# A two-layer decoder trunk: plain products for the seven-product units, token-major units of 512 columns, GpSimd's arithmetic on VectorE

## Chip, cores and metric

The kernel runs on one core of a Trainium2 chip. The metric is device time in microseconds for one launch, the median of several runs; a profile is one execution recorded instruction by instruction. TensorE (PE) multiplies matrices, VectorE (DVE) and ScalarE (ACT) do elementwise work and empty the accumulators, GpSimd (POOL) does elementwise work and issues some transfers, SyncE (SP) issues the rest.

## What is computed

Two layers over 512 tokens of width 1024. In each layer one input projection feeds five branches: A, sparse attention with a top-k choice of 128 keys; B, latent attention; C, differential attention; D, a spatial gating unit with a LayerNorm; E, attention into 256 memory rows. Each branch is gated, projected and merged, and the sum is projected and added to the rows:

```python
for l in range(DEPTH):
    xn = rms_norm(h, norm_g[l])
    (a_q, a_k, a_v, i_q, i_k, i_w, b_cq, b_ckv, b_kr, c_q, c_k, c_v,
     d_u, d_v, e_q, gates, merge) = jnp.split(xn @ w_in[l], offsets, axis=-1)
    branches = (dsa_branch(...), mla_branch(...), diff_branch(...), sgu_branch(...), memory_branch(...))
    mixed = functools.reduce(jnp.add, [
        jax.nn.sigmoid(merge[:, :, n]) * ((o * jax.nn.silu(gates[:, :, n])) @ w_branch[l, n])
        for n, o in enumerate(branches)])
    h = h + mixed @ w_out[l]
return rms_norm(h, final_norm_g)
```

## The kernel before, in words

**Products.** An fp32 operand is split into two fp32r parts, hi and lo. `three` (L484) issues three matmuls for one 128-row block: hi·hi, lo·hi, hi·lo; a "triple" below. Weights come in granules of 512 KB (`gcols`, four row blocks of 256 columns), loaded by SP. For each half granule `split_steps` (L392) lets ScalarE copy the hi part (L402) and an engine subtract it for the lo part (L405): VectorE the first half, GpSimd the second.

**Units.** `unit_t` (L489) makes 256 columns of a result transposed, columns on partitions and 512 tokens in the free dimension, so its matmuls are 512 wide; gates, merges and the branch projections use it. `unit_n` (L500) makes a token-major result: the rows are the stationary operand, the weights are moved, 256 columns at a time, for four token tiles. It makes the middle columns (keys, values, indexer, latent ranks), the queries of A (`a0 a1`), queries, keys and values of C in two halves (`f0q f0k f0v f1q f1k f1v`), the two inputs of D (`dv0 dv1 du0 du1`), the memory values and the output projection. `unit_s` (L509) makes the same block as `unit_t` from half blocks in seven sums of products in place of eight, 256 wide; `seven_steps` (L363) forms the combined weights, partly on GpSimd, and `x_prep` and `x_swap` (tokens `xp`, `xs`) the combined rows. Gates and merges of A and C use it, 12 units in each layer. Their sums stand in tile `s`, of the plain units in `pm`.

**Order.** The string `ORDER` (L31) lists units and marks. `gB0` is a half of branch B's gate, `mB0` a quarter of its merge (with its quarter of the branch projection); `+dsa` starts the side stream of the sparse attention, `-dsa` and `!df0` demand that one is done. `Pace` (L58) steps the side streams at each `tick` of a triple, by estimated times; `begin` splits weights ahead. The steps are recorded in this order and then placed on each engine's own queue by the framework; an engine runs its queue in order.

**Around the change.** The indexer of A (`+idx`) makes a score tile per block of 128 tokens and takes the top values with MAX (L1061) and MATCH_REPLACE (L1062) on VectorE, 16 pairs per block for blocks 1 to 3, while PE works on branch B's gates and merges and on `f0v`. Only when all are done the sparse attention goes on: a head multiplies scores (`pS`), takes a masked softmax (custom instruction L581, ScalarE L586, reciprocal L591, ScalarE L592), transposes (`pT`), splits (`ptl`) and multiplies values (`po`), for four blocks. LayerNorm of D (`ln`, L1259) works on the tile `sguv` and has its statistics and normalisation on VectorE, gain (L1271) and offset (L1272) on GpSimd, then a split into `vnh` and `vnl`, which the product `pz` of the token `z` needs. In `gates` GpSimd multiplies gate and branch output (L1375); in `merges` it adds into the accumulators (L1411).

Of the kernel before, what the change touches and what calls it, by code (L numbers as in the profile page):

```python
# [39 lines left out]
GSET = (1,)  # L40
WSB = True
STB = True
# [15 lines left out]
class Pace:  # L58
    """Interleaves side streams (attention) with the dense products as they are traced."""
# [68 lines left out]
class Granule:  # L128
    """Up to four 128-row blocks of 256 columns of a weight, split in two fp32r parts."""

    def __init__(self, parts, n, width=256, raws=1):
        self.parts, self.n, self.width, self.raws = parts, n, width, raws


def trunk(tc, d, out, taps=None):
# [43 lines left out]
    def f32(ap):  # L179
        return ap.bitcast(F32)  # L180
# [13 lines left out]
    # ---- input rows, small vectors, constants  # L194
# [59 lines left out]
    # ---- rotary tables  # L254
# [42 lines left out]
    def rope(eng, x, j, ct, st, outs=None):  # L297
        """x [128, 2, h, 2H], token tiles 2j and 2j+1; rotated in place or into outs."""
        h, w = x.shape[2], x.shape[3]
        hf = w // 2  # L300
        tmp = tr(name="rope")
        n = 2 * h * w
        a = tmp[:, :n] if 2 * n <= 512 else tr(name="rope2")[:, :n]
        b = tmp[:, n:2 * n] if 2 * n <= 512 else tmp[:, :n]
        a, b = (z.rearrange("p (t h w) -> p t h w", t=2, h=h) for z in (a, b))

        def tb(tab, lo, hi):
            return tab[:, 2 * j:2 * j + 2, None, lo:hi].to_broadcast([128, 2, h, hi - lo])
# [9 lines left out]
    # ---- differential lambdas  # L318
# [20 lines left out]
    # ---- long lived tiles  # L339
# [7 lines left out]
    # ---- weights  # L347
    order, state = [], {"dma": 0, "split": 0, "slot": 0}

    def issue(upto):  # L350
        while state["dma"] < min(upto, len(order)):
            g = order[state["dma"]]
            g.raw = [wp.tile([128, 4, 256], F32, tag="raw", bufs=NRAW, name="raw") for _ in range(g.raws)]
            for dst, src in g.parts(*g.raw):
                nc.sync.dma_start(dst, src)
            state["dma"] += 1
# [6 lines left out]
    def seven_steps(g):  # L363
        """Seven combinations of the four 512 x 128 blocks of a granule, split, in the order of their products."""
        r0, r1 = g.raw
        a11, a21, a12, a22 = (r[:, :, c * 128:(c + 1) * 128] for r in (r0, r1) for c in range(2))
        g.prod = []

        def put(src):
            h, lo = (z.rearrange("p (k c) -> p k c", k=4) for z in wtile())  # L370
            A.activation(h, src, AF.Copy)
            yield
            (G if len(g.prod) in GSET else V).tensor_tensor(out=lo, in0=src, in1=f32(h), op=ALU.subtract)  # L373
            g.prod.append((h, lo))
            yield

        def comb(x, y, op):
            o = (blk(F32, "ws") if WSB else pp.tile([128, 512], F32, tag="p", name="ws")).rearrange(
                "p (k c) -> p k c", k=4)
            G.tensor_tensor(out=o, in0=x, in1=y, op=op)  # L380
            return o
        yield from put(a11)
        s1 = comb(a21, a22, ALU.add)
        s2 = comb(s1, a11, ALU.subtract)
        yield from put(s2)
        yield from put(comb(a11, a21, ALU.subtract))
        yield from put(s1)
        yield from put(comb(a12, s2, ALU.subtract))
        yield from put(a22)
        yield from put(a12)  # L390
# [1217 lines left out]
```

## Time and profile before

| | before |
|---|---|
| median of 3 runs | 1853.85 us (1853.25 to 1854.87) |
| span of the profiled execution | 1854.6 us |
| instructions | 31211 |
| busy PE | 1784.2 us, 96% |
| busy VectorE | 1280.2 us, 69% |
| busy ScalarE | 1000.2 us, 54% |
| busy GpSimd | 730.9 us, 39% |
| PE on the chain that ended last | 42% of the span |
| read from HBM | 155.22 MB, 86 GB/s over the span |

The rows come from the page of one execution and from its trace. "L485 PE MATMUL pm<-wh,xh" is an instruction with its line, its output and its inputs; for a token-major product the weights `wh` are the moved operand. A duration belongs to one instruction; successive matmuls overlap, so that their distance is less than their duration. In a table of stretches each engine has its busy time and its number of instructions, and PEclk is the granted clock of TensorE, 1.00 being 2.4 GHz.

### The profile page before, as it was taken

What the parts mean: (1) busy time and instruction counts of PE and PEld (TensorE: products, weight loads), DVE (VectorE), ACT (ScalarE), POOL (GpSimd) and SP (SyncE); (2) the same over time, 40 slices, a digit from 0 to 9 for tenths busy, and PEclk for the clock granted to TensorE, in tenths of its full rate; (3) what the DMA queues carried; (4) which work ended last, traced back from release to release, by engine and by line L of the source; (5) the groups of instructions that cost most, each with busy time, mean ns of one, the idle gap of its engine ahead of it and who ended that gap; (6) DMA issues with size and microseconds to landing.
All of it is one profiled execution on the core that took longest, in us unless ns stands there. A gap on an engine that the chain in (4) does not pass through costs nothing. (4 is left out here: it accounts for less than half of the span.)

```text
span 1854.6 us, 31211 instructions
## 1 busy us (share of the span) xinstructions
PE 1784.2 (96%) x11481; PEld 1613.9 (87%) x11481; DVE 1280.2 (69%) x2979; ACT 1000.2 (54%) x2247; POOL 730.9 (39%) x603
## 2 busy tenths in 40 slices
PE   7999999999999997999999999999999999899898
PEld 6998889889988777989999988898999887789888
DVE  7438656996755679899354477489775655998963
ACT  7447766437745434455355567653476454444443
POOL 4123111442312366885241321125341133778733
PEclk9999999999999998999999999999999999999999
DMA  6322222332222222334452332223322222233241
GB/s 211 92 69 78 86 69 69 97 97 70 58 58 69 80 58 69 99 95 136 131 177 58 75 89 79 57 80 103 103 58 58 58 80 58 59 91 109 85 148 69
DMA packets 167745, 161.43 MB, mean 87 GB/s; under 512 B 26036, under 2 KB 163304, under 8 KB 167592
## 3 DMA queue, kind: packets, MB, share of 16 engines
q1 hardware_dynamic: 164648, 149.21, 28.0%
q0 software_dynamic: 2944, 10.23, 1.6%
q8 instruction: 91, 1.49, 0.3%
q14 instruction: 62, 0.51, 0.1%
HBM read 155.22 MB, written 4.19 MB: 86 GB/s over the span
## 5 line engine op out<-in xcount | busy, mean ns | idle before, releaser
L405 POOL TENSOR_TENSOR wl<-raw,wh 128x512 fp32r<-128x512 f32 (+1 forms) x226 | 300.8, 1332 | 803.8 <-ACT wh L402 632.8
L402 ACT ACTIVATE wh<-raw 128x512 fp32r<-128x512 f32 (+1 forms) x460 | 285.3, 623 | 328.1 <-PE pm L486 161.6
L485 PE MATMUL pm<-wh,xh 128*128 128x256 f32 x1024 | 294.6, 288 | 0.9 <-ACT nat L1091 0.8
L486 PE MATMUL pm<-wl,xh 128*128 128x256 f32 x1024 | 293.3, 286 | 0.0
L487 PE MATMUL pm<-wh,xl 128*128 128x256 f32 x1024 | 293.2, 286 | 0.0
L405 DVE TENSOR_TENSOR wl<-raw,wh 128x512 fp32r<-128x512 f32 (+1 forms) x234 | 182.7, 782 | 144.5 <-ACT wh L402 140.1
L485 PE MATMUL pm<-xh,wh 128*128 128x512 f32 x656 | 259.2, 396 | 0.8 <-ACT mth L1392 0.5
L487 PE MATMUL pm<-xh,wl 128*128 128x512 f32 x656 | 256.9, 394 | 0.0
L486 PE MATMUL pm<-xl,wh 128*128 128x512 f32 x656 | 256.7, 391 | 0.0
L485 PEld LDWEIGHTS pm<-wh,xh 128*128 128x128 f32 x1024 | 195.1, 190 | 5.8 <-ACT nat L1091 1.6
L487 PEld LDWEIGHTS pm<-wh,xl 128*128 128x128 f32 x1024 | 195.2, 191 | 2.8 <-issue 1.7
L486 PEld LDWEIGHTS pm<-wl,xh 128*128 128x128 f32 x1024 | 195.3, 191 | 2.7 <-issue 1.2
L586 ACT ACTIVATE p<-p,nm 128x512 f32<-128x512 f32 (+1 forms) x192 | 107.2, 558 | 78.2 <-DVE nm L584 77.3
L485 PEld LDWEIGHTS pm<-xh,wh 128*128 128x128 f32 x656 | 123.7, 189 | 26.8 <-ACT mth L1392 1.1
L487 PEld LDWEIGHTS pm<-xh,wl 128*128 128x128 f32 x656 | 123.6, 188 | 26.5
L486 PEld LDWEIGHTS pm<-xl,wh 128*128 128x128 f32 x656 | 123.7, 189 | 23.8
L485 PE MATMUL s<-xh,wh 128*128 128x256 f32 x384 | 113.1, 295 | 25.2 <-ACT mth L1392 12.2
L485 PE MATMUL pm<-yh,wh 128*128 128x512 f32 x320 | 125.9, 394 | 5.3 <-DVE st L528 5.3
L486 PE MATMUL pm<-yl,wh 128*128 128x512 f32 x320 | 126.0, 394 | 0.0
L487 PE MATMUL pm<-yh,wl 128*128 128x512 f32 x320 | 122.6, 392 | 0.0
L486 PE MATMUL s<-xl,wh 128*128 128x256 f32 x384 | 111.4, 290 | 0.0
L487 PE MATMUL s<-xh,wl 128*128 128x256 f32 x384 | 110.6, 291 | 0.0
(378 smaller groups left out, 4756.5 us busy)
## 6 DMA issues: line engine op xcount, KB each, us to landing
raw<-w_in SPq DMA_DIRECT2D x192, 512.0 KB, 3.7
raw<-w_branch SPq DMA_DIRECT2D x40, 512.0 KB, 3.5
raw<-mem_w_kv SPq DMA_DIRECT2D x16, 512.0 KB, 5.6
raw<-w_out SPq DMA_DIRECT2D x16, 512.0 KB, 3.7
raw<-mla_w_uq SPq DMA_DIRECT2D x18, 128.0 KB, 2.7
xrow<-x SPq DMA_DIRECT2D x4, 512.0 KB, 7.9
raw<-mla_w_ukv SPq DMA_DIRECT2D x16, 128.0 KB, 2.7
h<-x POOLq DMA_DIRECT2D x4, 512.0 KB, 4.6
```

The lines of the kernel that those rows point to most:

```text
L402: A.activation(hv, raw, AF.Copy)
L405: (G if a else V).tensor_tensor(out=lv, in0=raw, in1=f32(hv), op=ALU.subtract)
L485: T.matmul(o, ah, bh, start=st, stop=False)
L486: T.matmul(o, ah, bl, start=False, stop=False)
L487: T.matmul(o, al, bh, start=False, stop=sp)
L586: A.activation(p[:, :L], p[:, :L], AF.Exp, bias=nm, scale=scale, accum_out=s)
```

## The change

- `unit_s`, `seven_steps`, `gseven`, `x_prep`, `x_swap` and the tokens `xp` and `xs` go; gates and merges of A and C are plain `unit_t`.
- `unit_w` takes the place of nearly all `unit_n`: 512 columns at a time, one accumulator for each of the four token tiles, granules of two row blocks of 512 columns (`gwide`), a result handed on token tile by token tile. Four middle units become two, `a0 a1` become `a`, C's values `fv`, its queries and keys `f0` (256 query and 256 key columns) and `f1`; `dv`, `du`, the memory values and the first half of the output projection are single units too. The second half of it stays at 256.
- The second subtract of each granule, the gate product, the accumulator add, LayerNorm's gain and offset and the final gain go from GpSimd to VectorE.
- `fv` and `dv` stand ahead of `f0`; the pool of 512-column tiles has 35 instead of 36 buffers, that of short-lived ones 8 instead of 6.

```diff
-ORDER = ("-mem gE0 !ckvt !lat qr q0 !qr0 gE1 k0 v0 +mla0 mE0 q1 k1 mE1 -mla0 !qr1 v1 +mla1 mE2 mE3 a0 -mla1 +idx a1 "
-         "gB0 gB1 mB0 mB1 mB2 mB3 !aq +dsa ws f0v dv0 dv1 f0q f0k z du0 du1 -dsa !df0 +df0 f1q f1k f1v -df0 !oD !df1 "
-         "gD0 gD1 +df1 mD0 mD1 -df1 mD2 xp mD3 !xp xs gA0 gA1 mA0 mA1 mA3 mA2 gC0 gC1 mem mC0 mC1 mC3 mC2")
+ORDER = ("-mem gE0 !ckvt !lat qr q0 !qr0 gE1 k0 v0 +mla0 mE0 q1 k1 mE1 -mla0 !qr1 v1 +mla1 mE2 mE3 a -mla1 +idx "
+         "gB0 gB1 mB0 mB1 mB2 mB3 !aq +dsa ws fv dv f0 z du -dsa !df0 +df0 f1 -df0 !oD !df1 "
+         "gD0 gD1 +df1 mD0 mD1 -df1 mD2 mD3 gA0 gA1 mA0 mA1 mA3 mA2 gC0 gC1 mem mC0 mC1 mC3 mC2")
-NB = 36
+NB = 35
-NTR = 6
+NTR = 8
...
     def split_steps(g):
...
-        for a in range(0, g.n, 2):
+        for a in range(0, g.n, g.per):
...
-            (G if a else V).tensor_tensor(out=lv, in0=raw, in1=f32(hv), op=ALU.subtract)
+            V.tensor_tensor(out=lv, in0=raw, in1=f32(hv), op=ALU.subtract)
...
+    def gwide(w, k0, *c0s):
+        def parts(raw):
+            r = w[k0 * 128:(k0 + 2) * 128, :].rearrange("(k p) c -> p k c", p=128)
+            cw = 512 // len(c0s)
+            return [(raw[:, :, i * cw:(i + 1) * cw], r[:, :, c0:c0 + cw]) for i, c0 in enumerate(c0s)]
+        g = Granule(parts, 2, 512)
...
-    def unit_s(g, xb, evac):
-        """Transposed 256 columns by 512 tokens in seven products of half blocks instead of eight."""
...
+    def unit_w(gs, lh, ll, evac, nt=4):
+        def run():
+            ps = [None] * nt
+            for n, g in enumerate(gs):
+                begin(g)
+                for t in range(nt):
+                    if n == 0:
+                        ps[t] = psm()
+                    for a in range(2):
+                        kt = 2 * n + a
+                        three(ps[t], lh(kt, t), ll(kt, t), g.h[a][:, 0], g.l[a][:, 0], kt == 0, kt == 2 * len(gs) - 1)
+                        tick(3 * 512 * 0.43)
+                    if n == len(gs) - 1:
+                        evac(t, ps[t])
         plan.append(run)
...
+        def diff_v():
...
+            unit_w(ww(C_CV), tk(xh), tk(xl), ev)
...
-                    G.tensor_tensor(out=v, in0=v, in1=S["lng"], op=ALU.mult)
-                    G.tensor_tensor(out=v, in0=v, in1=S["lnb"], op=ALU.add)
+                    V.tensor_tensor(out=v, in0=v, in1=S["lng"], op=ALU.mult)
+                    V.tensor_tensor(out=v, in0=v, in1=S["lnb"], op=ALU.add)
...
-                    G.tensor_tensor(out=sg, in0=sg, in1=oT[nm][k], op=ALU.mult)
+                    V.tensor_tensor(out=sg, in0=sg, in1=oT[nm][k], op=ALU.mult)
...
-                if seven:
-                    unit_s(gseven(w, c0), xb, lambda ps, u=u: ev(ps, u))
-                else:
-                    unit_t(wg(c0), 8, xh_, xl_, lambda ps, u=u: ev(ps, u))
+                unit_t(wg(c0), 8, xh_, xl_, lambda ps, u=u: ev(ps, u))
...
                         if not first:
+                            V.tensor_tensor(out=acc[k], in0=acc[k], in1=dst, op=ALU.add)
                             if last:
-                                V.tensor_tensor(out=acc[k], in0=acc[k], in1=dst, op=ALU.add)
...
-                            else:
-                                G.tensor_tensor(out=acc[k], in0=acc[k], in1=dst, op=ALU.add)
...
-            if l == DEPTH - 1 and u < 3:
-                G.tensor_tensor(out=h, in0=h, in1=hs["g"][:, c], op=ALU.mult)
+            if l == DEPTH - 1 and n < 2:
+                V.tensor_tensor(out=h, in0=h, in1=hs["g"][:, c], op=ALU.mult)
...
-        for u in range(3):
...
+        unit_w([gwide(d["w_out"][l], k0, 0) for k0 in range(0, 8, 2)], lambda kt, t: mixed(kt, t)[0],
+               lambda kt, t: mixed(kt, t)[1], lambda t, o: residual(o, t, 0, 512, 0))
```

Three places of the order are spoken of below. Line numbers of the changed kernel are its own.

**Place one**, VectorE in the first layer, from the last steps of the top-k choice to the first softmax of the sparse attention (MAX and MATCH_REPLACE are the choice, wl weight subtracts, mth merges, ISA the masked softmax). Before:

```order
L1061 MAX m_4612<-score 128x8
L1062 MATCH_REPLACE score<-m_4612,score 128x512
L1061 MAX m_4625<-score 128x8
L1062 MATCH_REPLACE score<-m_4625,score 128x512
L405 TENSOR_TENSOR wl<-raw,wh 128x512
L1064 TENSOR_SCALAR score<-score 128x512
L1403 SCALAR_TENSOR_TENSOR mth<-mth,pm 128x512 x2
L405 TENSOR_TENSOR wl<-raw,wh 128x512
L581 ISA p,m<-pS,score 128x512
L581 ISA m 128x1
L584 TENSOR_SCALAR nm<-m 128x1
L591 RECIPROCAL r<-s 128x1
```

With the change:

```order
L1006 MATCH_REPLACE score<-m_4324,score 128x512
L1005 MAX m_4347<-score 128x8
L1006 MATCH_REPLACE score<-m_4347,score 128x512
L1005 MAX m_4360<-score 128x8
L1006 MATCH_REPLACE score<-m_4360,score 128x512
L371 TENSOR_TENSOR wl<-raw,wh 128x512 x2
L1005 MAX m_4373<-score 128x8
L1006 MATCH_REPLACE score<-m_4373,score 128x512
L1008 TENSOR_SCALAR score<-score 128x512
L543 ISA p,m<-pS,score 128x512
L543 ISA m 128x1
L546 TENSOR_SCALAR nm<-m 128x1
```

Two subtracts of one granule stand side by side among the steps of the choice, and the merges' instructions that stood between the last step and the softmax stand earlier.

**Place two**, VectorE in the first layer, where LayerNorm of branch D begins (BN_STATS and the tiles sguv, lng, lnb and vnl are LayerNorm's, ptl, ISA and r a sparse head's). Before, among the products of f0q and f0k:

```order
L1265 BN_STATS st<-sguv 128x6
L405 TENSOR_TENSOR wl<-raw,wh 128x512
L188 TENSOR_TENSOR ptl<-pT,pth 128x2x128
L1266 BN_AGGR mv<-st 128x2
L1268 TENSOR_SCALAR lr<-mv 128x1
L591 RECIPROCAL r<-s 128x1
L581 ISA p,m<-pS,score 128x384
L581 ISA m 128x1
L584 TENSOR_SCALAR nm<-m 128x1
L1270 TENSOR_SCALAR sguv<-sguv,mv,lr 128x512
L1265 BN_STATS st<-sguv 128x6
```

With the change, behind the last subtracts of f0, ahead of z:

```order
L1203 BN_STATS st<-sguv 128x6
L1204 BN_AGGR mv<-st 128x2
L1206 TENSOR_SCALAR lr<-mv 128x1
L1203 BN_STATS st<-sguv 128x6
L1208 TENSOR_SCALAR sguv<-sguv,mv,lr 128x512
L1204 BN_AGGR mv<-st 128x2
L1209 TENSOR_TENSOR sguv<-sguv,lng 128x512
L1206 TENSOR_SCALAR lr<-mv 128x1
L553 RECIPROCAL r<-s 128x1
L1210 TENSOR_TENSOR sguv<-sguv,lnb 128x512
L1208 TENSOR_SCALAR sguv<-sguv,mv,lr 128x512
```

The gain and offset steps (lng, lnb) are on VectorE's queue now, and the steps stand closer together.

**Place three**, PE in the first layer, at the scores of a first sparse head before, among the products of f0v:

```order
L1105 MATMUL pS<-kkh,qs 128x256
L1106 MATMUL pS<-kkl,qs 128x256
L485 MATMUL pm<-wh,xh_116 128x256
L486 MATMUL pm<-wl,xh_116 128x256
L487 MATMUL pm<-wh,xl_124 128x256
L485 MATMUL pm<-wh,xh_117 128x256
```

and with the change a head behind fv, up to the first product of dv (pS, po and pT are the head's, pm is the dense product):

```order
L563 MATMUL pT<-ident,p 128x128 x4
L1048 MATMUL pS<-kkh,qs 128x256
L1049 MATMUL pS<-kkl,qs 128x256
L563 MATMUL pT<-ident,p 128x128 x3
L1048 MATMUL pS<-kkh,qs 128x512
L1049 MATMUL pS<-kkl,qs 128x512
L563 MATMUL pT<-ident,p 128x128 x2
L1048 MATMUL pS<-kkh,qs 128x384
L1049 MATMUL pS<-kkl,qs 128x384
L563 MATMUL pT<-ident,p 128x128
L453 MATMUL pm<-wh,xh_115 128x512
```

The scores stood between dense products, and now two heads stand by themselves, of which this is the second.

## Rows read from the trace of the kernel before

**Rows 1.** The page, busy time of each engine (us, share of the span, instructions).

```profile
PE 1784.2 (96%) x11481; PEld 1613.9 (87%) x11481; DVE 1280.2 (69%) x2979; ACT 1000.2 (54%) x2247; POOL 730.9 (39%) x603
```

**Rows 2.** The timeline of PE, branch E's units: start us, busy us.

```profile
111.21 0.28 PE L485 MATMUL pm<-wh,xh 128*128 128x256 f32 x1
...
125.25 0.28 PE L485 MATMUL pm<-wh,xh 128*128 128x256 f32 x1
```

**Rows 3.** The timeline of PE, a plain stretch of branch B.

```profile
325.10 0.40 PE L485 MATMUL pm<-xh,wh 128*128 128x512 f32 x1
...
331.91 0.39 PE L485 MATMUL pm<-xh,wh 128*128 128x512 f32 x1
```

**Rows 4.** PE by form: shapes, count; busy us, mean ns; idle ahead.

```profile
L485 PE MATMUL pm<-wh,xh 128*128 128x256 f32 x1024 | 294.6, 288 | 0.9 <-ACT nat L1091 0.8
...
L485 PE MATMUL s<-xh,wh 128*128 128x256 f32 x384 | 113.1, 295 | 25.2 <-ACT mth L1392 12.2 <-DVE st L528 11.5 <-ACT wh L371 1.2
...
L485 PE MATMUL s<-t,wh 128*128 128x256 f32 x288 | 85.8, 298 | 10.5 <-DVE st L528 5.6 <-DVE mth L1403 4.9
...
L485 PE MATMUL pm<-wh,mxh 128*128 128x256 f32 x256 | 72.3, 283 | 0.0
```

**Rows 5.** Stretches: busy us of each engine, PEclk, DMA share, GB/s.

```profile
693.10:888.30 195.20, 177.47 (x1226) 167.16 (x1225) 172.21 (x245) 96.16 (x179) 138.01 (x95) 0.95 0.34 103
...
1603.70:1802.30 198.60, 175.27 (x1208) 164.89 (x1208) 170.33 (x228) 90.71 (x163) 136.89 (x90) 0.95 0.32 95
...
316.00:407.00 91.00, 91.00 (x409) 75.67 (x408) 88.25 (x196) 36.64 (x64) 41.41 (x32) 1.00 0.36 102
...
706.60:713.30 6.70, 6.70 (x46) 6.70 (x46) 6.05 (x9) 2.42 (x4) 6.08 (x5) 0.77 0.06 6
```

**Rows 6.** The top-k stretch: all engines, then tile score alone (columns as above).

```profile
319.00:408.40 89.40, 89.40 (x404) 74.46 (x403) 87.17 (x193) 34.43 (x60) 41.41 (x32) 1.00 0.35 101
...
319.00:408.40 89.40, 62.41 (x154) 1.00 0.35 101
```

**Rows 7.** The timeline of VectorE in the top-k stretch.

```profile
359.85 0.68 DVE L1403 SCALAR_TENSOR_TENSOR mth<-mth,pm 128x512 f32<-128x512 f32 x1
360.45 0.56 DVE L1061 MAX8 m<-score 128x8 f32<-128x384 f32 x1
```

**Rows 8.** All engines by form: the second weight subtract, plain and seven-product.

```profile
L405 POOL TENSOR_TENSOR wl<-raw,wh 128x512 fp32r<-128x512 f32 x216 | 293.5, 1360 | 776.9 <-ACT wh L402 605.9 <-issue 48.3 <-DVE p L751 19.6
...
L373 DVE TENSOR_TENSOR wl<-raw,wh 128x512 fp32r<-128x512 f32 x72 | 93.6, 1302 | 0.6 <-ACT wh L371 0.5
```

**Rows 9.** The timeline of PE, ahead of the top-k stretch.

```profile
317.04 0.28 PE L1049 MATMUL pI<-kil,iqs 128*128 128x256 f32 x1
```

**Rows 10.** The timeline of VectorE and ScalarE at the first sparse softmax.

```profile
411.76 0.68 DVE L581 CUSTOM_DVE_ANT_0 p<-pS,score 128x512 f32<-128x512 f32 x1
...
413.72 0.72 ACT L592 ACTIVATE p<-p,r 128x512 f32<-128x512 f32 x1 [0.23 <-DVE r L591]
```

**Rows 11.** VectorE, eight sparse heads, on tiles p, m, r, ptl and oA.

```profile
411.70:519.60 107.90, 15.35 (x32) 1.00 0.23 63
...
411.70:519.60 107.90, 7.42 (x64) 1.00 0.23 63
...
411.70:519.60 107.90, 5.06 (x32) 1.00 0.23 63
...
411.70:519.60 107.90, 15.52 (x32) 1.00 0.23 63
...
411.70:519.60 107.90, 5.44 (x8) 1.00 0.23 63
```

**Rows 12.** Instructions of tile sguv: duration ns min/median/max, start us, forms.

```profile
L1265 DVE BATCH_NORM_STATS2 st<-sguv x4: 684/685/689, 457.6 to 463.9; 128x6 f32<-128x512 f32 x4
...
L1270 DVE TENSOR_SCALAR sguv<-sguv,mv,lr x4: 547/811/1448, 460.2 to 470.0; 128x512 f32<-128x512 f32 x4
...
L188 DVE TENSOR_TENSOR vnl<-sguv,vnh x8: 407/419/1510, 468.6 to 481.7; 128x256 fp32r<-128x256 f32 x8
```

More of the change, by code (lines that the diff above doesn't have):

```diff
@@ L352, in issue @@
             g = order[state["dma"]]
-            g.raw = [wp.tile([128, 4, 256], F32, tag="raw", bufs=NRAW, name="raw") for _ in range(g.raws)]
-            for dst, src in g.parts(*g.raw):
+            raw = wp.tile([128, 1024], F32, tag="raw", bufs=NRAW, name="raw")
+            g.raw = raw.rearrange("p (k c) -> p k c", k=2 if g.per == 1 else 4)
+            for dst, src in g.parts(g.raw):
                 nc.sync.dma_start(dst, src)
@@ L361, in wtile @@
         return [wp.tile([128, 512], F32R, tag=f"{n}{i}", bufs=1, name=n) for n in ("wh", "wl")]
[L363 to L390, printed above, removed]
     def split_steps(g):
-        if g.raws == 2:
-            yield from seven_steps(g)
-            return
-        g.raw = g.raw[0]
         g.h, g.l = [], []
-        for a in range(0, g.n, 2):
-            b = min(a + 2, g.n)
-            h, lo = (z.rearrange("p (k c) -> p k c", k=2) for z in wtile())
+        for a in range(0, g.n, g.per):
+            b = min(a + g.per, g.n)
+            h, lo = (z.rearrange("p (k c) -> p k c", k=g.per) for z in wtile())
             raw, hv, lv = g.raw[:, a:b, :g.width], h[:, :b - a, :g.width], lo[:, :b - a, :g.width]
@@ L713, in wg, with ww @@
             return [gcols(w, k0, 4, c0) for k0 in (0, 4)]
+        def ww(*c0s):
+            return [gwide(w, k0, *c0s) for k0 in range(0, 8, 2)]
         for u in range(2):
@@ L1282, in z @@
                 pace.force("ws", "ln")
-                S["z"] = [blk(F32, "z").rearrange("p (g c k) -> p g c k", g=2, c=4) for _ in range(4)]
+                S["z"] = [c4(F32, "z").rearrange("p (c g k) -> p g c k", c=2, g=8) for _ in range(2)]
                 for gp in range(4):
@@ new lines, in ev, with post @@
+            def ev(t, o):
+                S["yD"].append(blk(F32, "yD"))
+                z = S["z"][t // 2].rearrange("p g c k -> p c g k")[:, t % 2]
+                V.tensor_tensor(out=S["yD"][t].rearrange("p (g k) -> p g k", g=8),
+                                in0=o.rearrange("p (g k) -> p g k", g=8), in1=z, op=ALU.mult)
+                if t == 3:
+                    pace.later(0.0, post(), "oD")
+            def post():
+                yield LAG_YD
+                for k in range(4):
+                    p = psa()
+                    for t in range(4):
+                        T.transpose(p[:, t * 128:(t + 1) * 128], S["yD"][t][:, k * 128:(k + 1) * 128], ident)
+                    oT["D"][k] = blk(F32, "oD")
+                    A.activation(oT["D"][k], p, AF.Copy)
+                    yield 700.0
@@ L1360, in layer, with d_v_unit, d_u_unit, gates @@
+            S["ev_u"] = ev
+        def d_v_unit():
+            unit_w(ww(C_DV), tk(xh), tk(xl), lambda t, o: S["ev_v"](t, o))
+        def d_u_unit():
+            unit_w(ww(C_DU), tk(xh), tk(xl), lambda t, o: S["ev_u"](t, o))
         y = {}
         M = {}
-        def gates(nm, us, seven=False):
+        def gates(nm, us):
             bi = "ABCDE".index(nm)
@@ L1378, in gates, with merges @@
                 c0 = C_GATE + 512 * bi + 256 * u
[L1379 to L1384 removed]
+                unit_t(wg(c0), 8, xh_, xl_, lambda ps, u=u: ev(ps, u))
+        def merges(nm, us, last=False):
             bi = "ABCDE".index(nm)
@@ L1456, in layer @@
             elif c == "g":
-                gates(a[0], (int(a[1]),), seven)
+                gates(a[0], (int(a[1]),))
             elif c == "m":
-                merges(a[0], (int(a[1]),), seven=seven, last=a[0] == "C")
+                merges(a[0], (int(a[1]),), last=a[0] == "C")
             elif tok == "qr":
@@ L1493, in load_h @@
                 nc.gpsimd.dma_start(hs["h"][t], src[t * 128:(t + 1) * 128, :])
-            hs["ss"] = [cp.tile([128, 4], F32, tag="hss", bufs=8, name="hss") for _ in range(4)]
+            hs["ss"] = [cp.tile([128, 3], F32, tag="hss", bufs=8, name="hss") for _ in range(4)]
             hs["g"] = None
```

332 lines of the change are left out of this document (107 added, 225 removed).

## The prediction

> **What bounds the kernel now.** I read the page's first part first: TensorE (PE) has work in 96% of the span [rows 1], so what counts is how closely its products follow each other and where it stands still. A matmul's busy time overlaps the next one's, so the timeline has to give the spacing. With 256 columns, 117 steps lie between the two rows of [rows 2]: 14.04 us / 117 = 0.120 us. With 512 columns, 30 steps lie between those of [rows 3]: 6.81 / 30 = 0.227 us. One wide product thus takes 0.227 us for the work of two narrow ones, 0.240.
>
> The list of forms gives the numbers to multiply with [rows 4]: 1024 triples of token-major products, 256 of the output projection, and 384 + 288 of the seven-product units (tile s). Then the table by stretches [rows 5]. Its first two rows are the stretches of branches A and C in the two layers, where the seven-product units work: PE is busy for 177.5 of 195.2 us and for 175.3 of 198.6, so it stands still for 41 us, and the mean granted clock is 0.95. In the third row, branch B's plain gates and merges, it is busy for all of 91.00 us at a clock of 1.00. In the fourth, shortly behind a halt, the mean is 0.77: part of it at the lower of the two levels (1.2 of 2.4 GHz). So dense plain stretches run without a gap, the seven-product stretches don't.
>
> **Plain units in branches A and C.** Removed: 24 seven-product units with their combinations on GpSimd, ScalarE and VectorE, and the preparation of the rows (xp, xs). Per unit 84 products of 256 columns go (10.1 us) and 48 of 512 come (10.9): over 24 units PE's own work grows by 19.6 us. But the two stretches measure 393.8 us [rows 5], and their work at the spacings is only 2016 × 0.120 + 384 × 0.227 + 1.9 (16 transposes at no more than a narrow product's time) = 331: 63 us are halts and low clock. As plain units the stretches hold 1536 × 0.227 + 1.9 = 350.6. **Gain 43.2.** The other end is four times branch B's 91.0 = 364, gain 29.8. I take the first: 1536 counts these stretches, and B's row holds side work that they lack. VectorE is no obstacle here: a plain merge has ten of its instructions of some 0.6 us beside 72 × 0.227 = 16.3 us of products. The preparation of the rows costs nothing by itself, being hidden by the products of mD2 and mD3 (0 to −3); were that cover gone, its halts are in the 63 already.
>
> **Wide token-major units.** 1024 triples, 128 of w_out's 256 (two of its four quarters) and, from the code, 64 of the memory values make 1216 × 3 = 3648 products × 0.120 = 437.8; now 1824 × 0.227 = 414.1. **Gain 23.7**; the lower end is 0, if the wide form takes what two narrow ones take. I go by the dense row. The Trainium skill, "TensorE: Matmul & The Clock Gate", section Back-to-back issue gap, has 262 cycles for 256 columns and 518 for 512, that is 0.109 and 0.216 us at the full clock; by that this term would be 4 us, and the whole 20 us later. The trace disagrees on the narrow form (0.120). The transfers cost nothing: a granule is one transfer of the same bytes as before, under products; without that cover it would be a wait for a single transfer.
>
> **GpSimd's arithmetic on VectorE, in the top-k stretch.** Here VectorE is full: from the first MAX to the last MATCH_REPLACE it is busy for 87.2 of 89.4 us, 62.4 of them on the score tile, and PE is busy throughout [rows 6]. In the changed order VectorE has 66 other instructions from that MAX to the first softmax of the sparse attention (35 weight subtracts instead of 16, 8 mth, 8 accumulator adds that were GpSimd's, 7 sg, 4 qs, 4 yl), all 512 columns wide. One alone takes 0.68, but the next instruction starts 0.60 behind it [rows 7]: 62.4 + 66 × 0.60 = 102. GpSimd's own share of subtracts took 1.36 us each, and VectorE's subtracts beside GpSimd's combinations 1.30 [rows 8]; the 0.60 supposes that this slowing is gone. On PE the second block's last indexer product starts at 317.04, 2.0 us ahead of the first MAX at 319.0 [rows 9]. From it to the first transposes of the sparse attention the changed order has 419 products of 512 columns (95.1 us) and some 5.2 of indexer, scores and transposes: 100.3. From the first softmax instruction to normalised rows it is 411.76 to 414.44 = 2.7, with 0.6 for the last compare 3.3 [rows 10]. PE waits for 2.0 + 102 + 3.3 − 100.3 = 7.
>
> Behind that, two heads of sparse attention stand on PE without a dense product between them. A head costs VectorE (15.35 + 7.42 + 5.06 + 15.52 + 5.44) / 8 = 6.1 us [rows 11], and PE 4 × (0.227 + 0.17 + 0.12 + 0.12) for scores and values and ten transposes at 0.12 or less, 3.7: 2 × 2.4, some 4 to 5. **Loss 11 per layer, 22 in all**; bounds 4 (only half of the added instructions are late) and 18 (all 66 at 0.68, and a third head).
>
> **LayerNorm at the end of f0.** GpSimd's two passes per token tile (1336 and 1422 ns) come to VectorE at some 0.69. A tile then costs it 0.685 (statistics), 0.5 of small steps, 0.55, 2 × 0.69 and 2 × 0.42 [rows 12]: 15 us for four. In the order these steps stand no more among the dense products but behind f0's softmaxes, ahead of z. From the softmax ahead of them to the last vnl VectorE has the 15, a head, and subtracts (7.5 together); up to the first pz PE has 21 dense products (4.8), 42 of attention and 27 transposes (some 9.8): 22.5 − 14.6 = 8, and 2 to 3 for a second bare head. **Loss 11 per layer, 22 in all**; bounds 0 (covered, as before) and 18.
>
> **The rest.** Behind four such halts the clock comes back late: 0.77 over 6.7 us [rows 5] is a loss of 1.5 to 2 each, **8** (4 to 13). The small units of k and v and the start now wait for both subtracts from one engine, some eight times 0.69: **6** (2 to 10). Gate product and final gain cost nothing beside the next unit's products; without them, at the very end, they would be 4 × 0.6.
>
> **Sum:** −43.2 − 23.7 + 22 + 22 + 8 + 6 = −8.9, from the profiled span of 1854.6 to 1845.7. That span is 0.75 above the median of the runs, 1853.85, so the forecast is **1845 us**. Taken as independent, the far ends (13.4, 23.7, 14, 14, 5, 4 above; 3, 14, 22, 4, 4 below) make 35 and 27: 1818 to 1880 is this case's own range.
>
> **Rival A: VectorE's backlog stays covered** (1793). No halt appears at fv or z: 1854.6 − 66.9 + 6 − 0.75. It happens if VectorE gets back more from a silent GpSimd than it takes over. For it: 1.30 against 0.68 us [rows 7, 8]. A rule of the Trainium skill, "SBUF — State Buffer", section Who interferes with whom, would bring it about: VectorE and GpSimd share a port pair, and a VectorE instruction with two SBUF inputs contends with a GpSimd one that reads SBUF. The trace agrees as to the slowing. Against it: in [rows 6] 62.4 + 33 others × 0.60 make 82 of the 87.2, so at most 5 us can come back there, for 33 more instructions, 20 us.
>
> **Rival B: slower, VectorE is the bound from the first MAX to du** (1873). The price is 18 us per layer at fv and 18 at z instead of 11 and 11: −8.9 + 28 = +19. It decides from 13.2 at each on, where the sum is 0. For it: 97% of VectorE is taken in [rows 6] before anything is added. Against: nearly the whole of it lies beside PE's own 100 us.
>
> **Rival C: the halts of branches A and C stay** with plain units, because they come from evictions and not from the combinations: 1853.85 + 19.6 − 23.7 + 58 = 1908. Against it: the same plain code without a gap in [rows 5].
>
> That the change doesn't do what it says is excluded by the order, which has 8793 products for 11481.
>
> **Chances.** Forecast 0.60, A 0.20, B 0.17, C 0.03. Some 0.2% (3.7 us) is what a measurement of this kernel can tell from no change: faster is below 1850.1, slower above 1857.6. Of the forecast case 0.6 lies below, 0.16 between and 0.24 above (a spread of 18 around 1845); A is all faster, B and C are slower: faster 0.36 + 0.20 = 0.56, same 0.10, slower 0.14 + 0.20 = 0.34. The range takes the own range, the upper half of A and most of B: 1796 to 1880, which leaves out 0.11 of A, 0.04 of B, all of C and 0.02 of the forecast.
>
> **What would show it.** In the changed profile: the stretches of A and C near 175 us each, PE busy throughout at a clock of 1.00; dense wide products 0.227 apart; PE idle for 5 to 10 us ahead of the first transposes behind fv, and for 5 to 12 ahead of pz, both released by VectorE. No halts there mean A; over 13 at each means B; halts in the gates and merges of A and C mean C. The forecast is wrong if wide products take 0.24, or if PE waits in places that the sum doesn't name.

## The result, and the profile after

The changed kernel takes 1888.08 us (median of 4 runs, 1887.75 to 1888.77) beside 1853.55: a ratio of 1.0182, interval 1.0167 to 1.0196. It is slower by 34 us where 9 less were forecast, and outside the range. The profiled execution has a span of 1885.7.

The page's first part and, below it, its row of TensorE's granted clock in 40 slices (tenths of full speed):

```profile
PE 1802.5 (96%) x8793; PEld 1489.3 (79%) x8793; DVE 1187.3 (63%) x3009; ACT 947.3 (50%) x2127; POOL 66.1 (4%) x133
...
PEclk9999999999989999999999999999998999999999
```

VectorE is less busy than before (1187 us for 1280 in [rows 1]), though it took over GpSimd's work: its weight subtracts of 512 columns take 689 ns each (542 of them) where VectorE needed 788 (230) and GpSimd 1360 (216). PE has 2688 fewer instructions and yet 18 us more busy time, at a clock that falls in two slices. The 96% hide what happened; stretches show it. Those below go from the first product of a unit to the first of another: f0v or fv up to gD, gD up to branch A, A and C of the first layer, A and C of the second. The table of stretches of the changed kernel (columns as in [rows 5]):

```profile
406.90:602.70 195.80, 175.29 (x826) 138.96 (x824) 129.76 (x391) 107.65 (x263) 3.77 (x6) 0.93 0.20 57
602.70:728.10 125.40, 121.00 (x560) 95.66 (x561) 76.78 (x244) 57.48 (x152) 10.72 (x18) 0.96 0.24 72
728.10:904.10 176.00, 176.00 (x786) 145.79 (x786) 87.61 (x143) 66.15 (x119) 3.49 (x6) 1.00 0.35 104
1660.10:1834.20 174.10, 174.10 (x770) 144.15 (x769) 82.23 (x127) 60.77 (x103) 2.21 (x5) 1.00 0.35 105
```

and of the kernel before, for the first three:

```profile
407.30:583.30 176.00, 174.36 (x1360) 166.12 (x1359) 114.07 (x394) 112.02 (x282) 46.18 (x40) 1.00 0.23 63
583.30:699.60 116.30, 108.58 (x508) 86.35 (x506) 78.30 (x195) 52.44 (x136) 52.58 (x43) 0.97 0.24 68
699.60:887.40 187.80, 176.16 (x1217) 166.26 (x1218) 164.81 (x230) 92.72 (x172) 136.06 (x93) 0.95 0.34 104
```

Branches A and C came out as forecast: 176.0 + 174.1 = 350.1 us with PE busy throughout at a clock of 1.00, against 393.8 in [rows 5]. The loss lies ahead of them: 195.8 for 176.0 and 125.4 for 116.3 us, and of the old 116.3 some 6 were the wait for the first seven-product unit, which is gone. From fv to A a layer takes 321 us instead of 292.

Where PE stands still there is seen in its timeline and in the lists of the tiles that the units leave behind. First PE in the changed kernel at fv's end, at the first product of dv, at f0's end, and at the first products of z and gD:

```profile
429.56 0.39 PE L455 MATMUL pm<-wh,xl 128*128 128x512 f32 x1
436.00 1.11 PE L563 MATMUL pT<-ident,p 128*128 128x128 f32 x4 [6.05 <-ACT p L554]
...
450.45 0.33 PE L563 MATMUL pT<-ident,p 128*128 128x128 f32 x1 [0.34 <-DVE dv L186]
450.53 0.47 PE L453 MATMUL pm<-wh,xh 128*128 128x512 f32 x1
...
508.13 0.40 PE L455 MATMUL pm<-wh,xl 128*128 128x512 f32 x1
...
532.62 0.56 PE L453 MATMUL pz<-vnh,wsh 128*128 128x256 f32 x1
...
602.66 0.79 PE L453 MATMUL pm<-xh,wh 128*128 128x512 f32 x1 [0.85 <-ACT nat L1013]
```

Then the instructions that take a result out of its accumulator (tile dv: fv's results; sguv: dv's; nat: f0's), and the last step of LayerNorm, vnl (durations min/median/max in ns, first and last start in us):

```profile
L185 ACT ACTIVATE dv<-pm x8: 378/384/399, 447.8 to 453.7; 128x256 fp32r<-128x256 f32 x8
L186 DVE TENSOR_TENSOR dv<-pm,dv x8: 414/418/425, 448.6 to 454.1; 128x256 fp32r<-128x256 f32 x8
...
L1192 ACT ACTIVATE sguv<-pm x4: 587/595/598, 475.4 to 479.8; 128x512 f32<-128x512 f32 x4
...
L186 DVE TENSOR_TENSOR vnl<-sguv,vnh x8: 389/416/424, 507.5 to 520.9; 128x256 fp32r<-128x256 f32 x8
...
L1013 ACT ACTIVATE nat<-pm x4: 597/620/687, 531.7 to 536.5; 128x512 f32<-128x512 f32 x4
```

Three things are to be seen. fv's last product starts at 429.56; PE waits 6.05 us for the first normalised rows of the sparse attention, which is the wait of 7 us that was forecast. But fv's results lie in the accumulators until 447.8 to 454.1, and dv begins at 450.53: until then PE has bare heads (and eight transposes of z's weights) and nothing else. f0's last product starts at 508.13, its results are taken away only from 531.7 on, and z begins at 532.62, while LayerNorm's last step was issued at 520.9. And gD's first product is released by the instruction that takes away a result of f1 (`nat`). The ring of accumulators has four members; a 512-wide unit fills all of them. The two stretches without a dense product, ahead of z and ahead of dv:

```profile
508.13:532.62 24.49, 15.82 (x54) 11.50 (x53) 19.98 (x67) 16.33 (x45) 1.10 (x2) 0.59 0.07 22
429.56:450.53 20.97, 11.89 (x52) 7.83 (x51) 15.13 (x53) 15.04 (x39) 0.00 (x0) 0.84 0.09 26
```

The narrow units before lose nothing there: in that trace f0v's results lie until 431.6 to 435.0 too, but dv0 starts at 423.32, 0.47 us behind f0v's last product (422.85), and dense products run on up to z with gaps of 3.1 us at most.

### The profile page after: what moved, and what is told of

The parts are those of the page before. It is cut to its first block, busy times and chain, and to the rows that moved or that the text cites. A ratio compares the mean times of both kernels' runs of the same rounds, so it can differ in the third digit from the quotient of the medians.

```text
span 1885.7 us, 24863 instructions
## 1 busy us (share of the span) xinstructions
PE 1802.5 (96%) x8793; PEld 1489.3 (79%) x8793; DVE 1187.3 (63%) x3009; ACT 947.3 (50%) x2127; POOL 66.1 (4%) x133
## 4 chain that ended last, share of the span: by engine, by line
PE 87%; DVE 7%; ACT 5%; issue 1%; DMA 0%; POOL 0%; POOLq 0%; SPq 0%; DVEq 0%; ACTq 0%
PE pm L453 25%; PE pm L454 25%; PE pm L455 25%; PE po L573 2%; PE pT L563 1%; PE pS L453 1%; DVE ptl L186 1%; DVE wl L371 1%; ACT p L548 1%; PE pS L454 1%; PE pS L455 1%; PE po L1135 1%; ACT p L554 1%; ACT pth L185 1%; PE pa L1020 1%
## 5 line engine op out<-in xcount | busy, mean ns | idle before, releaser
L371 DVE TENSOR_TENSOR wl<-raw,wh 128x512 fp32r<-128x512 f32 x556 | 376.2, 682 | 362.2 <-ACT wh L368 350.9
L368 ACT ACTIVATE wh<-raw 128x512 fp32r<-128x512 f32 x556 | 346.0, 625 | 512.5 <-PE pm L454 334.1
L453 PE MATMUL pm<-xh,wh 128*128 128x512 f32 x1040 | 410.3, 395 | 4.4 <-ACT nat L1013 1.7
L454 PE MATMUL pm<-xl,wh 128*128 128x512 f32 x1040 | 408.8, 393 | 0.0
L455 PE MATMUL pm<-xh,wl 128*128 128x512 f32 x1040 | 408.0, 393 | 0.0
L453 PE MATMUL pm<-wh,xh 128*128 128x512 f32 x512 | 202.1, 399 | 1.2 <-DVE acc L1304 1.2
L455 PE MATMUL pm<-wh,xl 128*128 128x512 f32 x512 | 202.5, 397 | 0.0
L454 PE MATMUL pm<-wl,xh 128*128 128x512 f32 x512 | 201.1, 393 | 0.0
L453 PEld LDWEIGHTS pm<-wh,xh 128*128 128x128 f32 x512 | 96.1, 188 | 22.3 <-issue 2.0
L454 PEld LDWEIGHTS pm<-wl,xh 128*128 128x128 f32 x512 | 96.3, 188 | 18.2
```

The lines of the kernel that those rows point to most:

```text
L368: A.activation(hv, raw, AF.Copy)
L371: V.tensor_tensor(out=lv, in0=raw, in1=f32(hv), op=ALU.subtract)
L453: T.matmul(o, ah, bh, start=st, stop=False)
L454: T.matmul(o, ah, bl, start=False, stop=False)
L455: T.matmul(o, al, bh, start=False, stop=sp)
```

## Experiments

Ratios are to the kernel before, run beside each; its median was between 1853.6 and 1856.2 us in these sets, so that differences of some 3 us between two sets are read from traces or not at all. Diffs are to the kernel named.

**GpSimd's work given back** (to the changed kernel).

```diff
-            V.tensor_tensor(out=lv, in0=raw, in1=f32(hv), op=ALU.subtract)
+            (G if a else V).tensor_tensor(out=lv, in0=raw, in1=f32(hv), op=ALU.subtract)
-                    V.tensor_tensor(out=v, in0=v, in1=S["lng"], op=ALU.mult)
-                    V.tensor_tensor(out=v, in0=v, in1=S["lnb"], op=ALU.add)
+                    G.tensor_tensor(out=v, in0=v, in1=S["lng"], op=ALU.mult)
+                    G.tensor_tensor(out=v, in0=v, in1=S["lnb"], op=ALU.add)
-                    V.tensor_tensor(out=sg, in0=sg, in1=oT[nm][k], op=ALU.mult)
+                    G.tensor_tensor(out=sg, in0=sg, in1=oT[nm][k], op=ALU.mult)
-                            V.tensor_tensor(out=acc[k], in0=acc[k], in1=dst, op=ALU.add)
+                            (V if last else G).tensor_tensor(out=acc[k], in0=acc[k], in1=dst, op=ALU.add)
```

> The changed kernel with GpSimd's arithmetic given back: second subtract, gate product, accumulator add, LayerNorm's gain and offset. Theory V (the arithmetic on VectorE makes the sparse attention late, and PE's halts from fv to mD with it): the halts between fv and the end of mD shrink from some 55 us in a layer to about 20, as before the change; 1805 to 1825 us. Theory W (the wide units leave too few places in which side work can be interleaved): the halts stay, 1870 to 1890 us.

1883.4 us, ratio 1.0147 (1.0126 to 1.0168). Theory V is out as the cause of the whole: with all that arithmetic back, some 5 us are won. The first stretch in the table and the tile dv:

```profile
410.70:602.70 192.00, 173.98 (x825) 137.96 (x823) 116.03 (x346) 107.08 (x263) 43.31 (x36) 0.95 0.20 59
```

```profile
L185 ACT ACTIVATE dv<-pm x8: 372/380/386, 446.3 to 452.3; 128x256 fp32r<-128x256 f32 x8
```

fv's results still wait until 446.3, and the stretch is 192.0 us. The arithmetic does move a halt: dv starts 9.5 us behind fv's last product (439.43 to 448.88) instead of 21.0. But z starts 24.1 us behind f0's last (507.60 to 531.70), as in the changed kernel.

**The subtract alone given back**: the first two lines of that diff.

> The changed kernel with the second weight subtract alone back on GpSimd. Theory V, as a matter of the number of VectorE's instructions in the top-k stretch (19 of the 33 added ones there are subtracts): 60 to 80 per cent of what giving all of it back brings. Theory W: 1870 to 1890 us. If it is LayerNorm's steps that matter, less than a third of it.

1890.8 us, ratio 1.0188 (1.0173 to 1.0203): no gain. As all of the arithmetic together brings only some 5 us, the run can't tell whether counted instructions share it out.

**Plain units alone** (in the kernel before).

```diff
-gD0 gD1 +df1 mD0 mD1 -df1 mD2 xp mD3 !xp xs gA0
+gD0 gD1 +df1 mD0 mD1 -df1 mD2 mD3 gA0
```

> The kernel before with nothing but plain units in branches A and C (no seven products, no combined rows). Both theories: the two stretches take 175 us each with PE busy throughout, 1853.5 - 43 = 1811 us. If halts come up there from evictions: over 1850 us.

1812.98 us, ratio 0.9764 (0.9750 to 0.9779): 43 us less than the kernel before beside it (1856.02), where 43.2 were forecast. Its stretches from f0v to gD and from gD to A, f0v's results, and PE at the first product of dv0:

```profile
405.60:581.50 175.90, 174.51 (x1359) 166.13 (x1358) 114.02 (x394) 112.01 (x282) 45.89 (x40) 1.00 0.22 63
581.50:690.00 108.50, 106.87 (x508) 85.36 (x507) 54.08 (x163) 49.51 (x125) 42.84 (x40) 1.00 0.27 84
```

```profile
L187 ACT ACTIVATE dv<-pm x4: 378/382/385, 429.8 to 433.2; 128x256 fp32r<-128x256 f32 x4
```

```profile
421.52 0.28 PE L485 MATMUL pm<-wh,xh 128*128 128x256 f32 x1
```

f0v's results are late here as well, by 8 to 12 us. But dv0 starts at 421.52, ahead of them, since a narrow unit leaves two accumulators free.

**GpSimd's arithmetic on VectorE alone** (in the kernel before: the lines of the first diff the other way, and the final gain).

> The kernel before with nothing but GpSimd's arithmetic on VectorE (seven products and narrow units stay, GpSimd keeps the seven-product combinations). Theory V: halts come up from f0v to mD as in the changed kernel, 30 to 60 us slower, 1885 to 1915 us. Theory W: within 10 us of 1853.5.

1898.6 us, ratio 1.0233 (1.0214 to 1.0252), within theory V's range. But the loss has two places: f0v to gD takes 14 us longer in each layer, and A and C take 203.0 and 200.0 us instead of 187.8 and 191.4, with the seven-product combinations still there. So it was split again.

**The same with plain units in A and C.**

> The kernel before with plain units in A and C and with GpSimd's arithmetic on VectorE, units still 256 wide. From the run with the arithmetic moved alone (halts from f0v to f1 grow by 15 us in each layer, in gD and mD by nothing, the rest of its loss lies in the seven-product stretches): 1813 + 32 = 1845 us. If the loss of that run belongs wholly to the seven-product units: 1815 us.

1842.5 us, ratio 0.9937 (0.9918 to 0.9956), 29 us over the plain kernel, as expected:

```profile
403.40:593.00 189.60, 177.86 (x1347) 167.29 (x1346) 133.87 (x442) 111.62 (x278) 6.19 (x10) 0.96 0.19 57
```

Moving the arithmetic costs 29 us with narrow units and 5 with wide ones: in the wide kernel with GpSimd's work back PE stands still in the same stretch (192.0 us) for another reason.

**The order alone** (in the plain kernel).

```diff
-ws f0v dv0 dv1 f0q f0k z du0 du1 -dsa !df0 +df0 f1q f1k f1v -df0
+ws f0v f1v dv0 dv1 f0q f0k z du0 du1 -dsa !df0 +df0 f1q f1k -df0
```

> The kernel before with plain units in A and C (1813 us), and the 256-wide units between the sparse attention's start and its end in the order of the changed kernel: both halves of C's values ahead of D's first input. Theory O (that order strips the sparse attention of its dense cover): 1840 to 1880 us. Theory P (a 512-wide unit takes all four accumulators of the ring, so that nothing of the next unit can start before its results are taken away): within 8 us of 1813.

1834.1 us, ratio 0.9884 (0.9869 to 0.9899): +22 us, between the two expectations, so order is a part. Its stretches up to gD and up to A:

```profile
406.70:578.40 171.70, 169.70 (x1313) 161.13 (x1312) 107.63 (x359) 106.06 (x262) 44.13 (x37) 1.00 0.22 64
578.40:700.80 122.40, 117.68 (x554) 92.87 (x554) 59.86 (x196) 56.01 (x145) 44.31 (x43) 0.99 0.25 76
```

Up to gD it is even 4 us shorter, but gD and mD take 122.4 for 108.5: f1v had covered the first differential attention, which now runs over into gD (its last values product `po` starts 27 us behind gD's first, where it was 5). The changed kernel's 125.4 lies near; two runs below, with f1v at its old place, show whether it is the order or the width.

**Two accumulators for narrow units** (in the plain kernel), and **five for wide ones** (in the run with GpSimd's work back).

```diff
-        return psp.tile([128, 512], F32, tag="m", bufs=4, name=name)
+        return psp.tile([128, 512], F32, tag="m", bufs=2, name=name)
```

> The kernel before with plain units in A and C (1813 us), with two accumulators in the ring instead of four, so that a 256-wide unit takes all of them as a 512-wide one does in the changed kernel. Theory P: halts at the ends of units, above all where VectorE or ScalarE is behind (mid, f0v, d, f0): 1850 us or more. Theory O: within 15 us of 1813.

1892.9 us, ratio 1.0199 (1.0181 to 1.0216): 80 us slower than with four. Among its waits of PE, summed (what waited, for what: us, times, longest), are the releasers of theory P, instructions that empty accumulators (sg, nat, kl), for a small part of the 80 us:

```profile
PE pm L485 <- DVE sg L1374: 5.6, 8, 0.8
...
PE pm L485 <- ACT nat L1091: 4.4, 6, 1.3
PE pm L485 <- DVE kl L188: 3.5, 2, 1.8
```

The halts are spread over all units, those of gates and merges too, and are not gathered at f0v and f0 as in the changed kernel: f0v to gD takes 182.7 for 175.9 us, and 18 us of the loss in each layer lie in the stretch of the small units (from 131.4 to 303.7, for 128.6 to 282.7). So the run shows that units that fill the ring cost time; it doesn't show what that costs at fv and f0.

```diff
-        return psp.tile([128, 512], F32, tag="m", bufs=4, name=name)
+        return psp.tile([128, 512], F32, tag="m", bufs=5, name=name)
-        return psp.tile([128, 512], F32, tag="a", bufs=3, name=name)
+        return psp.tile([128, 512], F32, tag="a", bufs=2, name=name)
```

> The changed kernel with GpSimd's arithmetic given back (1883 us), with five accumulators in the ring and two instead of three for the side streams. Theory P: a spare accumulator lets the next unit start, the halts at the ends of mid, fv and f0 shrink by half or more, 1840 to 1865 us, unless the missing one of the side streams takes it back. Theory O: 1875 to 1895 us.

1957.4 us, ratio 1.0548 (1.0532 to 1.0564). The side streams lose more by their third accumulator than the wide units gain by a fifth, so the time tells nothing on P. The trace does, at z: with a spare accumulator it starts 10 us ahead of the first of f0's results, where in the changed kernel it starts behind it. It goes with LayerNorm's last steps now (vnl until 552.4), still 31 us behind f0's last product (521.25). At dv the trace shows nothing of the kind: dv starts at 472.97, behind the first of fv's results at 470.1.

```profile
552.08 0.58 PE L453 MATMUL pz<-vnh,wsh 128*128 128x256 f32 x1
...
L1013 ACT ACTIVATE nat<-pm x4: 597/632/646, 562.4 to 567.3; 128x512 f32<-128x512 f32 x4
```

**Other orders of the wide units** (in the changed kernel `dv fv f0 z`, then `dv f0 fv z`; the latter also with GpSimd's work back).

> The changed kernel (1888 us) with one swap in the order: D's first input dv ahead of C's values fv. dv's results are taken away by ScalarE alone and fv's by VectorE too, and LayerNorm has another unit ahead of z. Theory P (fv's results, waiting behind VectorE's queue in all four accumulators, keep the next unit from starting; LayerNorm then comes late): the halt behind the top-k stretch loses its two bare heads and the one ahead of z shrinks, 10 to 20 us in each layer, 1850 to 1870 us. If VectorE's work as such is the bound there: 1880 to 1895 us.

> The changed kernel with the order dv f0 fv z: fv no longer stands where VectorE is full, and LayerNorm has f0 and fv ahead of z. Theory P: the halts of the sparse attention go but for the wait of 7 us for the top-k choice, 1840 to 1860 us. If VectorE's work as such is the bound: 1880 to 1895 us.

> The changed kernel with GpSimd's arithmetic given back (1883 us) and the order dv f0 fv z. Theory P: 1825 to 1850 us, since the wait for the top-k choice goes too. If the wide units as such (fewer places for side work) are the cause: 1870 to 1885 us.

1876.95 (1.0113, 1.0096 to 1.0130), 1888.4 (1.0177, 1.0161 to 1.0193) and 1887.75 us (1.0171, 1.0156 to 1.0186). Three misses: the halts move to the end of whatever wide unit is under way while the heads run. In the first, f0 waits for fv's results and z for f0's; in the second and third, fv waits for f0's and z for fv's. None of the orders takes them away. The second time lies in the range of VectorE as the bound; the third, with GpSimd's work back and no faster, speaks against that. The first separates the accumulators from LayerNorm, which is done at 486.1 there, ahead of f0's last product (508.32); z starts at 527.47, with the first of f0's results (526.8):

```profile
L186 DVE TENSOR_TENSOR vnl<-sguv,vnh x8: 392/416/425, 472.2 to 486.1; 128x256 fp32r<-128x256 f32 x8
...
L1013 ACT ACTIVATE nat<-pm x4: 592/611/663, 526.8 to 532.4; 128x512 f32<-128x512 f32 x4
...
527.47 0.39 PE L453 MATMUL pz<-vnh,wsh 128*128 128x256 f32 x1 [0.98 <-ACT nat L1013]
```

**Wide units one by one.** In the plain kernel first the output projection's first half, then D's inputs too, then C's queries and keys.

> The kernel before with plain units in A and C (1813 us), of the wide units only the first half of the output projection, where no side stream runs. From the changed kernel's own stretch there (44.8 instead of 46.1 us in each layer): 1810 us. By P no halt, since results are taken away one token tile after another and VectorE is idle; if four accumulators hurt even here: 1815 us or more.

1809.9 us, ratio 0.9750 (0.9736 to 0.9765): some 3 us better than plain alone, which is no more than the noise, but the traces agree: from the first to the last product of the projection it is 44.7 instead of 46.0 us in each layer, 2.6 in all. Where nothing holds results back, the wide unit gains what it should.

```diff
-f0v dv0 dv1 f0q f0k z du0 du1
+f0v dv f0q f0k z du
```

> The kernel before with plain units in A and C and the wide first half of the output projection (1810 us), and with D's two inputs as 512-wide units too. In the changed kernel their results are taken away by the end of the unit (dv by 480.4 against 479.3 us, du by 564.1 against 563.0), since no side stream's work stands ahead of them. Theory P: no new halts, 4 x (192 x 0.120 - 96 x 0.227) = 5 us less, 1805 us. If wide units thin out the cover of the sparse attention as such (theory T): 1815 to 1840 us.

1821.6 us, ratio 0.9826 (0.9809 to 0.9842), 12 us worse instead of 5 better, and in theory T's range, which the run doesn't exclude. For P the expectation looked only at D's own results. A wide unit also needs the accumulators of the unit ahead of it: f0v's are freed between 431.9 and 436.0 (tile dv of that run), dv does 30 of its 96 products, breaks off at 428.72 and goes on at 434.52.

```diff
-f0v dv f0q f0k z du -dsa !df0 +df0 f1q f1k f1v
+f0v dv f0 z du -dsa !df0 +df0 f1 f1v
```

(with the pools' sizes of the changed kernel, 35 and 8.)

> The run before this one (1805 us expected) with C's queries and keys as 512-wide units f0 and f1 as in the changed kernel; C's values stay 256 wide at their places. Theory P: f0's and f1's results wait behind the sparse and the differential heads on ScalarE's queue, and z and the next unit with them: 10 to 20 us in each layer, 1825 to 1845 us. If only the order (both halves of the values early) and GpSimd's arithmetic matter: 1800 to 1810 us.

1829.6 us, ratio 0.9864 (0.9850 to 0.9879): 8 us more, where 20 to 40 were expected; the time falls in the range only because the run before had lost 12. The added time is in the stretch up to gD (184.5 for 179.7 us). From gD to A it is 109.5, with f0 and f1 wide but f1v at its old place.

**Narrow units for C in the changed kernel.**

```diff
-ws fv dv f0 z du -dsa !df0 +df0 f1 -df0
+ws f0v dv f0q f0k z du -dsa !df0 +df0 f1q f1k f1v -df0
```

> The changed kernel (1888 us) with C's queries, keys and values as 256-wide units in their old order; all else as changed, GpSimd's arithmetic on VectorE too. Theory P: what is left are the arithmetic's own 30 us and the halts of the middle columns (some 10), less the gain of the wide units that stay: 1840 to 1855 us. If the wide units' share of the loss is spread over all of them: 1860 to 1880 us.

1860.4 us, ratio 1.0032 (1.0020 to 1.0044): 28 us back of the 75 between the plain kernel and the changed one. The time is 5 us over P's range and in the other one (the loss spread over all wide units). And the edit changes two things, width and order: of the first layer's gain 10.6 us lie from gD to A (114.8 for 125.4), where f1v covers the differential attention again, and 2.5 from f0v to gD (193.3). With the run before, this puts the loss in gD and mD down to the order rather than to the width. dv is still wide and waits for f0v's results, which go 13 us later here, with GpSimd's arithmetic on VectorE, than in the run with D's inputs wide (431.9):

```profile
L185 ACT ACTIVATE dv<-pm x4: 378/384/399, 445.3 to 448.7; 128x256 fp32r<-128x256 f32 x4
```

**The heads started behind fv** (in the changed kernel).

```diff
-!aq +dsa ws fv dv f0 z du
+!aq ws fv +dsa dv f0 z du
```

> The changed kernel (1888 us) with the start of the sparse attention moved behind fv in the order, so that no head's instruction stands ahead of fv's results on VectorE's and ScalarE's queues. Theory P: fv's results are taken away within 3 us of its last product (21 us in the changed kernel), dv follows at once, and the halt of 14 us behind fv goes in each layer; what the later heads then lack in cover may take some of it back: 1855 to 1870 us. If the results are late for want of VectorE's time and not for their place in the queue: they stay 10 us or more late, 1880 us or more.

1862.8 us, ratio 1.0047 (1.0031 to 1.0064): −25 us by a move of one mark. fv's results, PE at the first product of dv, and the first stretch:

```profile
L185 ACT ACTIVATE dv<-pm x8: 367/382/388, 425.1 to 441.4; 128x256 fp32r<-128x256 f32 x8
```

```profile
430.05 0.40 PE L453 MATMUL pm<-wh,xh 128*128 128x512 f32 x1
```

```profile
406.30:588.20 181.90, 168.97 (x829) 134.76 (x828) 126.94 (x392) 106.82 (x263) 3.41 (x6) 0.99 0.21 61
```

The first results go at 425.1 instead of 447.8, dv starts at 430.05 instead of 450.53, 1.3 us behind fv's last product (428.78), and the stretch is 13.9 us shorter. The last of the eight still goes at 441.4, behind a head, and dv breaks off for it (440.05 to 442.63). VectorE has the same work as in the changed kernel; so fv's results were late for their place in the queues, behind the heads' instructions, and not for want of VectorE's time. From gD to A nothing is won (125.4).

**What beats both** is the run with plain units in A and C and only the output projection's first half wide: 1809.9 us.

## Why the prediction was wrong

- **Plain units, −43.2: right.** Alone they gave −43, and in the changed kernel the stretches are 350.1 us against 350.6 worked out.
- **Wide units, −23.7: right as PE's own work, wrong as an effect.** The output projection gained its share: 2.6 us, where 384 products × 0.120 less 192 × 0.227 make 2.5. (The Trainium skill, "TensorE: Matmul & The Clock Gate", section Back-to-back issue gap, would have 0.5 by its cycles for a single product; the trace goes with the rows. For the whole term these cycles make 4.6, not 4.) This is the step that failed: beside that gain the term weighed only the transfers, which "cost nothing", and put the wide units' other cost at nothing. It counted columns and granules and left out what a unit holds. Four accumulators of four mean that the next unit waits for the results of the last one. With GpSimd's work back, wide units and their order cost 70 us (1813 to 1883) in place of the gain of 23.7.
- **GpSimd's arithmetic, 7 us of waiting and 4 to 5 for two bare heads: the wait right (6.05 us), the cause of the bare heads missed.** The changed order showed them, with no dense product between. I read that as a gap of cover and priced it by what a head costs VectorE; it was the sign that dv's first product could not be placed earlier, since its accumulator was held. They last from 436.00 until dv's first product at 450.53, 14.5 us. As an effect the moved arithmetic costs 29 us with narrow units and 5 with wide ones.
- **LayerNorm at the end of f0, 11 us a layer: right for half of the halt, the other half missed.** LayerNorm's last step is issued at 520.9, 12.8 us behind f0's last product, near the 11; z starts 11.7 later still, at 532.62, right behind the first of f0's results at 531.7. The second half is the accumulators'. Nor is LayerNorm late by its own steps on VectorE: with gain and offset back on GpSimd its last step is issued at 524.6, 17 us behind f0's last product, and the stretch keeps 192.0 of 195.8 us. (The figures that the prediction gives for four tiles add up to 15.8, not 15.)
- **Not in the sum: gD and mD.** That fv takes f1v with it, ahead of the sparse attention, was named in the change and not priced. The order alone costs 22 us in the plain kernel: 14 more in gD and mD and 4 less ahead of them in the first layer.
- **Clock.** The mean was 0.93 in the stretch from fv to gD, and 0.59 over the 24.5 us ahead of z, so the lower clock behind the halts came as assumed, only more of it.
- **Small units of k and v, and the start, 6: nearly.** From E's gate behind the middle columns to A's queries a layer takes 156.2 us instead of 154.1, 4 in all; what of it is the subtracts' is not shown. The start is not longer: the middle columns begin at 64.2 instead of 69.5 us.
- **Rivals.** The time is 15 us over rival B's 1873, but its mechanism, VectorE as the bound from the first MAX to du, does not decide from fv on. VectorE is busy for 129.8 of 195.8 us there, though for 20.0 of the 24.5 ahead of z; with GpSimd's work back it is busy for 116.0, and the stretch keeps 192.0. Rival A is out, C too. The one that mattered, accumulators, was not among them. The signs that were named could not tell it: PE's idle time is 6.05 us ahead of the first transposes and 8.7 in all between f0 and z, within the forecast's 5 to 10 and 5 to 12, while the dense products stand 21.0 and 24.5 apart.

What is settled: with wide units dense products wait for results that stand behind the heads in ScalarE's and VectorE's queues (rows of the changed kernel; dv ahead of fv; the heads started later). By place, nearly all of the 75 us between the plain kernel and the changed one lie from fv to A: 20 in each layer up to gD, and 17 and 15 from gD to A, where the order explains 14 and 12. What was not tried is a wide unit that leaves an accumulator free without taking one from the side streams. How the 20 up to gD divide between accumulators and arithmetic has no single answer, as the parts overlap: over the whole kernel wide units with their order cost 70 alone, the arithmetic 29 alone, and both together 75.

## What to carry to other kernels

Before a unit is made wider, count the accumulators that it holds and look where the results of the unit ahead are taken away: a narrow unit that leaves half the ring free hides results that are 10 us late, a wide one turns them into a halt. In an order of instructions, side work that stands without dense work beside it is a symptom; ask which buffer kept the dense work from standing there. Work that is taken from one stretch to another takes its cover along.

## What the runs showed that was not expected

The clock fell without a long halt. From f1's last product (596.41) to 601.40 PE had worked on attention alone, with gaps of 0.56 and 0.49 us, at a granted clock of 1.00 up to 601.0. Over the 8.6 us from 601.40 on, in which it was busy for 7.75 and waited once, for 0.85 us ahead of gD's first product (602.66), the mean granted clock is 0.60, so most of them at the lower level of 1.2 GHz:

```profile
596.50:601.00 4.50, 3.45 (x27) 2.65 (x25) 3.91 (x17) 3.00 (x10) 0.55 (x1) 1.00 0.41 118
601.40:610.00 8.60, 7.75 (x25) 5.97 (x24) 6.85 (x34) 4.07 (x15) 1.22 (x2) 0.60 0.00 0
```

VectorE's single subtracts became faster with GpSimd silent (689 ns, against 788; with narrow units 688, against 760), but that took no time off the kernel: with narrow units the move cost 29 us all the same. The Trainium skill, "SBUF — State Buffer", section Who interferes with whom, has a VectorE instruction with two SBUF inputs contend with a GpSimd one that reads SBUF; these durations agree with it.
